# Expert gathers of a decoder block in sets of eight, with the rows of v fetched later and summed one at a time

## The chip, the cores and the metric

One core of a Trainium2 chip runs the whole kernel as one program. The metric is the device time of one execution in microseconds (us); lower is better. The core has five engines that each work through their own instructions in order: PE (matrix multiply), DVE (vector work), ACT (activations and copies), POOL (here it issues gathers) and SP (here it issues loads). DMA engines move data between the chip's memory and the core.

## What is computed

The reference is one layer of a decoder. It normalises the 1024 tokens, runs three attention branches on them, gates and adds the branches, projects, and then applies an expert layer. The change touches only the expert layer. Every token chooses 8 x 16 = 128 of 16384 experts, and an expert is one row of `u` and one row of `v`, of 1024 numbers each:

```python
def peer_ffn(h, w_q, subkeys, u, v):
    ...
    def chunk(args):
        hc, ic, gc = args
        act = jax.nn.gelu(jnp.einsum('chkd,cd->chk', u[ic], hc).astype(jnp.float32), approximate=False)
        w = (gc * act).astype(h.dtype)
        return jnp.einsum('chk,chkd->cd', w, v[ic])
```

So for each token and each of its experts: a dot product of the expert's `u` row with the token, GELU, a gate, and the `v` row times that number added to the token's output.

## The kernel before

The tokens form eight tiles of 128. Two of them (4 and 6) are done densely: `dense()` multiplies them with all 16384 experts, 128 experts at a time, in matmuls at L1221 (`uh`, `ul`, `hh`, `hl` for the dot products, `vh`, `vl`, `wh`, `wl` for the sums). For the other six tiles the rows are gathered. A gather fetches 128 rows, 0.5 MB: of 32 tokens, 4 experts each. A tile takes 128 gathers of `u` and 128 of `v`, so there are 768 of each, all issued by POOL at L1123.

`Experts.step` handles one gather. A gather of `u` lands in one of `UP` = 5 row buffers. At L1177 DVE multiplies it with the tokens' rows `hb` and sums it into one column of `parts`. `hb` holds each token's row once for every expert; `spread_rows` makes it for four gathers at a time with two matmuls into `pb` (L1116) and two copies on ACT (L128). The gather of `v` for the same experts is issued in the same step and lands in one of `VP` = 6 buffers.

Four gathers make a set. In the step after a set's last dot product, ACT takes the GELU of the set's four columns (`gel`); a step later DVE multiplies by the gates (L1191) and spreads the four columns into the weights `wz` (L1192); a step later PE does all four sums at once, 16 matmuls into `po` (L1203). These have 32 output rows each, so that four of them use a quarter of the array's columns each (`128*32` in the profile). A list called `behind` holds what the coming steps still have to do for a set. After 32 gathers, DVE adds `po` to the residual row and ACT issues the store of `row` (L1208, L1210).

ACT needs one table for `Exp` and `Ln` and another for `Gelu` and `Tanh`; when the next function needs the other table, an `ACT_TABLE_LOAD` is issued ahead of it (L126). Attention uses `Exp` and `Ln` throughout.

The program is one long stream. Attention, projections, the choice of experts and the dense part are a generator called the filler; the loop at its end puts one expert step after so much filler, by fixed costs (`LEAST`, `SLOW`, `TOKEN_NS`). The order of instructions of one engine is set when the program is built: ACT keeps the order in which the code is written, on the other engines a scheduler may move instructions by a little. In the order of PE the filler goes first through attention of the first group of tokens, then gates and projections, then the same for the next groups, then the gate matrix of the dense tiles, then the dense part, and behind that only expert steps are left.

Of the kernel before, what the change touches and what calls it, by code (L numbers as in the profile page):

```python
# [40 lines left out]
LEAST = 3000.0  # L41
SPLIT = (0,)
AHEAD = 2
UP, VP = 5, 6
GMAX = max(GROUPS)
NMAX = GMAX * 128

# [30 lines left out]
def block_kernel(ctx: ExitStack, tc: tile.TileContext, io):  # L78
# [1010 lines left out]
    def quarters(dram_tile, c):  # L1089

        return [dram_tile[32 * c:32 * c + 32, 256 * k:256 * k + 256] for k in range(4)]

    class Experts:
# [65 lines left out]
        def step(self):  # L1159

            self.supply()
            n, gT, box, g, i, ap = self.todo.pop(0)
            c, jj = divmod(g, QB)
            if i == 0:
                if jj == 4:
                    row = box["row"] = gw.tile([128, 256], F32, name="row", bufs=1)
                    for k, src in enumerate(quarters(xres[n], c)):
                        nc.sync.dma_start(row[32 * k:32 * k + 32], src)
                    if c < 3:
                        box["b"] = rows_of(n, c + 1)  # L1170
                self.spread_rows(n, box, g)
                self.hb = self.hbs.pop((n, g))
                self.parts = gw.tile([128, 4], F32, name="parts")
            self.run_behind()
            self.fetch("v", ap)
            u = self.us.pop(0)
            nc.vector.scalar_tensor_tensor(u, u, 1.0, self.hb, op0=OP.mult, op1=OP.mult,  # L1177
                                           accum_out=self.parts[:, i:i + 1])
            if i == 2 and self.todo[1:]:
                m, _, near, h, j, _ = self.todo[1]  # L1180
                if j == 0:
                    self.spread_rows(m, near, h)
            if i == 3:
                ge = gw.tile([128, 4], F32, name="gel")
                wz = gw.tile([128, 4, 32], F32, name="wz")

                def gelu(ge=ge, parts=self.parts):
                    actf(ge, parts, AF.Gelu)

                def weights(ge=ge, wz=wz):  # L1190
                    nc.vector.tensor_mul(ge, ge, gT[:, c, jj, :])  # L1191
                    nc.vector.tensor_mul(wz, ge[:, :, None].to_broadcast([128, 4, 32]),  # L1192
                                         spread[:, jj, None, :].to_broadcast([128, 4, 32]))

                def sums(i, wz=wz, box=box):
                    if "po" not in box:
                        box["po"] = pg.tile([128, 512], F32, name="po")
                    po = box["po"]
                    v = self.vs.pop(0)

                    h = 256 * (c % 2)
                    for k in range(4):
                        nc.tensor.matmul(po[32 * k:32 * k + 32, h:h + 256], wz[:, i, :],  # L1203
                                         v[:, 256 * k:256 * k + 256], start=jj == 0 and i == 0,
                                         stop=jj == QB - 1 and i == 3, skip_group_check=True)
                    if jj == QB - 1 and i == 3:
                        row = box["row"]
                        nc.vector.tensor_add(row, row, po[:, h:h + 256])  # L1208
                        for k, dst in enumerate(quarters(io["out"][n], c)):
                            nc.scalar.dma_start(dst, row[32 * k:32 * k + 32])  # L1210
                self.behind.append([gelu, weights, lambda: [sums(x) for x in range(4)]])
            return g == 31 and i == 3

        def flush(self):
# [308 lines left out]
```

## Time and profile before

| what | us |
|---|---|
| median of three runs (3707.89 to 3709.02) | 3708.14 |
| the profiled execution | 3714.9 |
| its span, first to last instruction | 3713.1 |
| PE busy | 3251.4 |
| DVE busy | 2341.3 |
| POOL busy | 1760.5 |
| ACT busy | 1354.4 |

The profiled execution took 0.18% longer than the median of the runs. PE is busy for 88% of the span and the 16 DMA engines carry 319 GB/s in the mean, but neither is an average of one kind of work: the stages differ. Attention with gathers beside it runs at 464 to 1021 us and at 1392 to 2042 us, gates and projections at 1021 to 1392 and 2042 to 2413, the gate matrix at 2413 to 2877, the dense part at 2877 to 3609, and expert steps alone from 3609 to the end. A row of a view that groups instructions has the line, the engine, the operation, the tiles as written and read, the count, and then busy time and the mean of one in ns; behind the second bar stands how long the engine was idle just before, and what ended that. For the sums (L1203) one matmul of the program is two records in the profile, so one gather is 8 records and a set of four 32.

### The profile page before, as it was taken

How to read it: one execution, taken by the hardware profiler on the slowest of the kernel's cores; microseconds unless marked ns; L12 is line 12 of the kernel's file. 1: busy time of each engine (PE TensorE's matmuls, PEld its weight loads, DVE VectorE, ACT ScalarE, POOL GpSimd, SP SyncE). 2: the span in 40 equal slices, each digit the busy share in tenths (PEclk: the TensorE clock that was granted, in tenths of full speed). 3: DMA queues.
4: the chain of work that ended last, by engine and by line, in shares of the span. 5: the costliest groups of instructions: out<-in, count | busy, mean ns of one | idle time of the engine just before them, and what ended most of it. 6: DMA issues, size and time to landing. Idle time of an engine off the chain costs nothing.

```text
span 3713.1 us, 60915 instructions
## 1 busy us (share of the span) xinstructions
PE 3251.4 (88%) x22802; PEld 2393.0 (64%) x22802; DVE 2341.3 (63%) x6153; ACT 1354.4 (36%) x2729; POOL 1760.5 (47%) x1544
## 2 busy tenths in 40 slices
PE   7999978988899888888888999875877999999984
PEld 7889755655555765655555656763556888888850
DVE  5443686455444468886555556589875777777664
ACT  4442235444311214555444222211223444444430
POOL 0000046645465455655444556445663555545556
PEclk9999989999999999999998999997988999999995
DMA  4345578889799998888977999988999999999999
GB/s 165 115 125 168 200 256 321 321 301 328 275 383 379 377 365 293 316 296 283 333 274 276 338 360 383 372 293 282 410 360 385 393 389 408 396 397 402 373 339 343
DMA packets 346431, 1185.55 MB, mean 319 GB/s; under 512 B 38744, under 2 KB 80216, under 8 KB 326680
## 3 DMA queue, kind: packets, MB, share of 16 engines
q0 software_dynamic: 221184, 805.40, 58.1%
q1 hardware_dynamic: 102672, 337.95, 24.8%
q10 hardware_dynamic: 22280, 38.31, 2.8%
q8 instruction: 180, 2.95, 0.3%
q14 instruction: 115, 0.94, 0.1%
HBM read 1142.18 MB, written 39.32 MB: 318 GB/s over the span
## 4 chain that ended last, share of the span: by engine, by line
PE 53%; DVE 16%; DMA 11%; issue 10%; ACT 4%; another core or an unknown queue 3%; POOL 3%; ACTq 1%; SPq 0%; POOLq 0%; DVEq 0%
PE bank L117 27%; PE bank L1221 17%; PE po L1203 6%; DVE u L1177 5%; DMA u<-in_u,iT 4%; DMA v<-in_v,iT 2%; POOL u L1123 1%; POOL v L1123 1%; PE pb L1116 1%; DMA b3d<-sp 1%; PE bank L121 1%; ACT e L128 1%; DMA ur<-in_uT 1%; DMA gd<-g 1%
## 5 line engine op out<-in xcount | busy, mean ns | idle before, releaser
L1123 POOL DMA_INDIRECT u<-in_u,iT x768 | 922.4, 1201 | 1137.2 <-DVE wide L339 476.9
L1123 POOL DMA_INDIRECT v<-in_v,iT x768 | 837.3, 1090 | 804.7 <-PE po L1203 588.5
L1177 DVE SCALAR_TENSOR_TENSOR u<-u,hb 128x1024 f32<-128x1024 f32 x768 | 922.9, 1221 | 465.6 <-ACT hb L128 232.7
L1203 PE MATMUL po<-v,wz 128*32 128x256 f32 x6144 | 436.6, 413 | 134.9 <-DVE wz L1192 72.4
L117 PE MATMUL bank<-wide,w 128*128 128x384 f32 x1536 | 523.5, 495 | 6.7 <-DVE sc L966 3.0
L117 PEld LDWEIGHTS bank<-wide,w 128*128 128x128 f32 x1536 | 294.4, 194 | 209.2 <-issue 19.2
L128 ACT ACTIVATE hb<-pb 128x512 f32<-128x512 f32 x384 | 209.8, 595 | 541.4 <-PE pb L1116 237.0
L1203 PEld LDWEIGHTS po<-v,wz 128*32 128x32 f32 x6144 | 184.4, 115 | 341.1 <-DVE wz L1192 93.9
L117 PE MATMUL bank<-w,wide 128*128 128x128 f32 x2304 | 273.7, 278 | 15.9 <-issue 11.7
L117 PEld LDWEIGHTS bank<-w,wide 128*128 128x128 f32 x2304 | 268.3, 194 | 25.9 <-issue 17.5
L117 PE MATMUL bank<-big,w 128*128 128x256 f32 (+1 forms) x1280 | 239.9, 343 | 8.4 <-issue 6.9
L1221 PE MATMUL bank<-hh,uh 128*128 128x256 f32 x848 | 242.7, 286 | 3.8 <-ACT uh L128 3.8
L1221 PE MATMUL bank<-hh,ul 128*128 128x256 f32 x848 | 241.0, 284 | 0.4 <-DVE ul L1301 0.4
L1221 PE MATMUL bank<-hl,uh 128*128 128x256 f32 x848 | 240.7, 284 | 0.0
L117 PEld LDWEIGHTS bank<-big,w 128*128 128x128 f32 x1280 | 209.2, 194 | 37.9 <-issue 14.0
L128 ACT ACTIVATE e<-bank 128x512 f32<-128x512 f32 (+2 forms) x208 | 109.5, 527 | 328.7 <-PE bank L117 232.7
L1221 PE MATMUL bank<-vl,wh 128*128 128x512 f32 x512 | 204.1, 399 | 10.9 <-DVE vl L1301 10.1
L1221 PE MATMUL bank<-vh,wh 128*128 128x512 f32 x512 | 203.8, 407 | 3.7 <-ACT vh L128 3.2
L1221 PE MATMUL bank<-vh,wl 128*128 128x512 f32 x512 | 200.8, 392 | 0.0
L126 ACT ACT_TABLE_LOAD x144 | 184.8, 1283 | 20.6 <-issue 12.1
L1301 DVE TENSOR_TENSOR vl<-vr,vh 128x1024 fp32r<-128x1024 f32 x128 | 157.1, 1227 | 34.0 <-ACT vh L128 28.0
L128 ACT ACTIVATE w<-bank 128x256 f32<-128x256 f32 x128 | 49.2, 385 | 336.3 <-PE bank L1221 255.0
(298 smaller groups left out, 5747.1 us busy)
## 6 DMA issues: line engine op xcount, KB each, us to landing
ur<-in_uT SPq DMA_DIRECT2D x64, 1024.0 KB
vr<-in_vd SPq DMA_DIRECT2D x64, 1024.0 KB
w<-in_w_in SPq DMA_DIRECT2D x102, 512.0 KB
w<-in_w_gate SPq DMA_DIRECT2D x72, 512.0 KB
w<-in_w_pq SPq DMA_DIRECT2D x48, 512.0 KB
g<-gd SPq DMA_DIRECT2D x16, 1024.0 KB
w<-in_w_o SPq DMA_DIRECT2D x48, 256.0 KB
w<-in_w_out SPq DMA_DIRECT2D x24, 512.0 KB
```

The lines of the kernel that those rows point to most:

```text
L117: nc.tensor.matmul(out, lhsT, rhs, **kw)
L121: nc.tensor.transpose(out, in_, ident)
L126: nc.scalar.preload_act_table_set(s)
L128: nc.scalar.activation(out, in_, f, **kw)
L1116: nc.tensor.matmul(pb, which[:, jj].rearrange("p q s -> p (q s)"), box["b3"][:, f], start=True, stop=True)
L1123: nc.gpsimd.indirect_dma_start(out=t, out_offset=None, in_=io[kind], in_offset=bass.IndirectOffsetOnAxis(ap=ap, axis=0))
L1177: nc.vector.scalar_tensor_tensor(u, u, 1.0, self.hb, op0=OP.mult, op1=OP.mult, accum_out=self.parts[:, i:i + 1])
L1203: nc.tensor.matmul(po[32 * k:32 * k + 32, h:h + 256], wz[:, i, :], v[:, 256 * k:256 * k + 256], start=jj == 0 and i == 0, stop=jj == QB - ...
L1221: nc.tensor.matmul(out, lhsT, rhs, **kw)
L1301: nc.vector.tensor_sub(lo, r[:, x], hi)
```

## The change

A set is now eight gathers. The column tile `parts` and the GELU tile `gel` have eight columns; GELU and the multiplication by the gates run once for eight gathers. The weights `wz` are still made four at a time, the second four of a set four steps after the first. The gather of `v` is issued six steps after its own `u` was used (`VLAG`), and its sum, four matmuls, runs ten steps after (`SLAG`), one gather in each step. There are six buffers for `u` and five for `v`.

```diff
-UP, VP = 5, 6
+UP, VP = 6, 5
+VLAG, SLAG = 6, 10
...
-                self.parts = gw.tile([128, 4], F32, name="parts")
+                if jj % 2 == 0:
+                    self.parts = gw.tile([128, 8], F32, name="parts")
             self.run_behind()
-            self.fetch("v", ap)
             u = self.us.pop(0)
+            at = 4 * (jj % 2) + i
             nc.vector.scalar_tensor_tensor(u, u, 1.0, self.hb, op0=OP.mult, op1=OP.mult,
-                                           accum_out=self.parts[:, i:i + 1])
+                                           accum_out=self.parts[:, at:at + 1])
...
+            def sums(at=at, i=i, jj=jj, c=c, box=box, now=self.set):
...
+                for k in range(4):
+                    nc.tensor.matmul(po[32 * k:32 * k + 32, h:h + 256], now[at // 4][:, i, :],
+                                     v[:, 256 * k:256 * k + 256], start=jj == 0 and i == 0,
+                                     stop=jj == QB - 1 and i == 3, skip_group_check=True)
...
+            self.behind.append([None] * (VLAG - 1) + [lambda ap=ap: self.fetch("v", ap)]
+                               + [None] * (SLAG - VLAG - 1) + [sums])
+            if at == 7:
+                ge = gw.tile([128, 8], F32, name="gel")
 
-                def weights(ge=ge, wz=wz):
-                    nc.vector.tensor_mul(ge, ge, gT[:, c, jj, :])
-                    nc.vector.tensor_mul(wz, ge[:, :, None].to_broadcast([128, 4, 32]),
-                                         spread[:, jj, None, :].to_broadcast([128, 4, 32]))
...
-                self.behind.append([gelu, weights, lambda: [sums(x) for x in range(4)]])
+                def scale(ge=ge, j0=jj - 1):
+                    nc.vector.tensor_mul(ge, ge, gT[:, c, j0:j0 + 2, :].rearrange("p j i -> p (j i)"))
+
+                def weights(z, ge=ge, now=self.set, j0=jj - 1):
+                    wz = now[z] = gw.tile([128, 4, 32], F32, name="wz")
+                    nc.vector.tensor_mul(wz, ge[:, 4 * z:4 * z + 4, None].to_broadcast([128, 4, 32]),
+                                         spread[:, j0 + z, None, :].to_broadcast([128, 4, 32]))
+                self.behind.insert(0, [gelu, lambda: (scale(), weights(0)), None, None, None, lambda: weights(1)])
```

Lines from 44 on are numbered one higher in the changed kernel, and later ones differ more: the sums are L1196 there, the dense matmuls L1229.

How often each engine does what, counted over the whole order of each engine:

| | before | changed |
|---|---|---|
| gathers of u, of v (POOL) | 768, 768 | 768, 768 |
| GELU of expert columns (ACT) | 192 | 96 |
| table loads (ACT) | 145 | 81 |
| products with the gates (DVE) | 192 | 96 |
| weights wz (DVE) | 192 | 192 |
| sums into po (PE, matmuls) | 3072 | 3072 |
| unbroken runs of such matmuls (PE) | 239 | 584 |
| of these ahead of the dense sums | 193 | 430 |
| among the dense sums | 39 | 147 |
| behind the last dense matmul | 7 | 7 |
| gathers summed behind the last dense matmul | 40 | 45 |

Ahead of each place of the filler the same `spread_rows` matmuls stand as before, so the steps are dealt out alike; the sums stand later.

On PE, in the dense part, before: a set of four sums stands in one piece between dense matmuls (`bank`), followed by the two `pb` matmuls for a coming set. The number behind a name tells one tile from the next.

```order
L1221 MATMUL bank_21896<-vl_26845,wh_26838 128x512
L1221 MATMUL bank_21896<-vh_26844,wl_26839 128x512
L1203 MATMUL po_25907<-v_26654,wz_26804 32x256 x4
L1203 MATMUL po_25907<-v_26746,wz_26804 32x256 x4
L1203 MATMUL po_25907<-v_26782,wz_26804 32x256 x4
L1203 MATMUL po_25907<-v_26800,wz_26804 32x256 x4
L1116 LDWEIGHTS which_83
L1116 MATMUL pb_26947<-b3_25375,which_83 128x512
```

The same engine in the dense part of the changed kernel: two sums of one gather each, with dense matmuls between them.

```order
L1229 MATMUL bank_21507<-vh_29601,wl_29596 128x512
L1196 MATMUL po_25754<-v_29500,wz_29494 32x256 x4
L1229 MATMUL bank_21504<-vh_29633,wh_29629 128x512
L1229 MATMUL bank_21504<-vl_29634,wh_29629 128x512
L1229 MATMUL bank_21504<-vh_29633,wl_29630 128x512
L1229 MATMUL bank_21505<-vh_29633,wh_29629 128x512
L1229 MATMUL bank_21505<-vl_29634,wh_29629 128x512
L1229 MATMUL bank_21505<-vh_29633,wl_29630 128x512
L1196 MATMUL po_25754<-v_29530,wz_29652 32x256 x4
L1117 LDWEIGHTS which_83
```

Where one run of sixteen matmuls stood, there are now runs of four at several places.

On ACT, in attention of the second group, before: two sets of four, each with a table load ahead of its GELU and another ahead of the next `rs` (which is `Ln` and then `Exp`).

```order
L126 ACT_TABLE_LOAD
L128 ACTIVATE gel_15180<-parts_15041 128x4
L128 ACTIVATE sq_15204<-bank_15195 128x384
L128 ACTIVATE hb_15234<-pb_15235 128x512
L128 ACTIVATE hb_15234<-pb_15238 128x512
L128 ACTIVATE sq_15252<-bank_15243 128x384
L126 ACT_TABLE_LOAD
L128 ACTIVATE rs_15256<-bank_15254 128x384
L128 ACTIVATE rs_15256<-rs_15256 128x384
L128 ACTIVATE sq_15257<-rs_15256 128x384
L126 ACT_TABLE_LOAD
L128 ACTIVATE gel_15272<-parts_15184 128x4
```

ACT at the same place of the changed kernel:

```order
L129 ACTIVATE sq_14890<-rs_14889 128x384
L129 ACTIVATE sq_14930<-bank_14921 128x384
L129 ACTIVATE hb_14952<-pb_14953 128x512
L129 ACTIVATE hb_14952<-pb_14956 128x512
L129 ACTIVATE sq_14970<-bank_14961 128x384
L129 ACTIVATE rs_14974<-bank_14972 128x384
L129 ACTIVATE rs_14974<-rs_14974 128x384
L129 ACTIVATE sq_14975<-rs_14974 128x384
L127 ACT_TABLE_LOAD
L129 ACTIVATE gel_14993<-parts_14772 128x8
```

One GELU of four columns and the pair of loads around it are gone.

On POOL, around the first gathers of the third gathered tile (its index tile is iT_11455), before: the v of a tile follows its u by five gathers of u.

```order
L1123 DMA u_11768<-in_u,iT_11455 128x1024
L1123 DMA v_11773<-in_v,iT_5663 128x1024
L1123 DMA u_11813<-in_u,iT_11455 128x1024
L1123 DMA v_11817<-in_v,iT_5663 128x1024
L1123 DMA u_11843<-in_u,iT_11455 128x1024
L1123 DMA v_11861<-in_v,iT_5663 128x1024
L1123 DMA u_11871<-in_u,iT_11455 128x1024
L1123 DMA v_11873<-in_v,iT_5663 128x1024
L1123 DMA u_11909<-in_u,iT_11455 128x1024
L1123 DMA v_11914<-in_v,iT_11455 128x1024
```

POOL at the same place of the changed kernel (the tile's index is iT_11277): five gathers of u into the tile, the gathers of v are still those of the tile before.

```order
L1124 DMA u_11565<-in_u,iT_11277 128x1024
L1124 DMA v_11571<-in_v,iT_5593 128x1024
L1124 DMA u_11574<-in_u,iT_11277 128x1024
L1124 DMA v_11580<-in_v,iT_5593 128x1024
L1124 DMA u_11619<-in_u,iT_11277 128x1024
L1124 DMA v_11627<-in_v,iT_5593 128x1024
L1124 DMA u_11653<-in_u,iT_11277 128x1024
L1124 DMA v_11659<-in_v,iT_5593 128x1024
L1124 DMA u_11669<-in_u,iT_11277 128x1024
L1124 DMA v_11675<-in_v,iT_5593 128x1024
```

The lead of u over v on POOL has grown by seven gathers: one from the deeper u buffers and six from the later fetch of v.

More of the change, by code (lines that the diff above doesn't have):

```diff
@@ L1182, in step @@
                     self.spread_rows(m, near, h)
[L1183 to L1187, printed above, removed]
-                    actf(ge, parts, AF.Gelu)
-                def weights(ge=ge, wz=wz):
-                    nc.vector.tensor_mul(ge, ge, gT[:, c, jj, :])
-                    nc.vector.tensor_mul(wz, ge[:, :, None].to_broadcast([128, 4, 32]),
-                                         spread[:, jj, None, :].to_broadcast([128, 4, 32]))
[L1195 to L1210, printed above, removed]
-                self.behind.append([gelu, weights, lambda: [sums(x) for x in range(4)]])
@@ new lines, in step @@
+            if at == 0:
+                self.set = {}
+            def sums(at=at, i=i, jj=jj, c=c, box=box, now=self.set):
+                if "po" not in box:
+                    box["po"] = pg.tile([128, 512], F32, name="po")
+                po = box["po"]
+                v = self.vs.pop(0)
+                h = 256 * (c % 2)
+                for k in range(4):
+                    nc.tensor.matmul(po[32 * k:32 * k + 32, h:h + 256], now[at // 4][:, i, :],
+                                     v[:, 256 * k:256 * k + 256], start=jj == 0 and i == 0,
+                                     stop=jj == QB - 1 and i == 3, skip_group_check=True)
+                if jj == QB - 1 and i == 3:
+                    row = box["row"]
+                    nc.vector.tensor_add(row, row, po[:, h:h + 256])
+                    for k, dst in enumerate(quarters(io["out"][n], c)):
+                        nc.scalar.dma_start(dst, row[32 * k:32 * k + 32])
@@ new lines, in step, with gelu @@
+            self.behind.append([None] * (VLAG - 1) + [lambda ap=ap: self.fetch("v", ap)]
+                               + [None] * (SLAG - VLAG - 1) + [sums])
+            if at == 7:
+                ge = gw.tile([128, 8], F32, name="gel")
+                def gelu(ge=ge, parts=self.parts, j0=jj - 1):
+                    actf(ge, parts, AF.Gelu)
+                def scale(ge=ge, j0=jj - 1):
[5 more added lines that the diff above has]
+                self.behind.insert(0, [gelu, lambda: (scale(), weights(0)), None, None, None, lambda: weights(1)])
```

## The prediction

> **What bounds the kernel now.** I read the page first, then the stretches stage by stage, then the waits, and last single moments in the order of time.
>
> ```profile
> PE 3251.4 (88%) x22802; PEld 2393.0 (64%) x22802; DVE 2341.3 (63%) x6153; ACT 1354.4 (36%) x2729; POOL 1760.5 (47%) x1544
> PE 53%; DVE 16%; DMA 11%; issue 10%; ACT 4%; another core or an unknown queue 3%; POOL 3%; ACTq 1%; SPq 0%; POOLq 0%; DVEq 0%
> ```
>
> PE is busiest (first row), and the chain of waits runs through it for half the span (second row). The rest of that chain is the loop of the expert steps and of attention through DVE, DMA and ACT. The stretches by stage show where each limit holds; their columns are the stretch, its length, busy time of PE, PEld, DVE, ACT and POOL with counts, granted clock, DMA share and GB/s.
>
> ```profile
> 464.00:1021.00 557.00, 479.08 (x3439) 313.82 (x3439) 331.77 (x884) 244.99 (x453) 297.06 (x267) 0.93 0.83 300
> 1021.00:1392.00 371.00, 337.11 (x2167) 233.62 (x2164) 183.27 (x457) 66.25 (x163) 213.00 (x196) 0.96 0.99 376
> 1392.00:2042.00 650.00, 560.89 (x4079) 370.62 (x4078) 444.57 (x1288) 318.30 (x572) 340.67 (x309) 0.93 0.83 296
> 2042.00:2413.00 371.00, 348.46 (x2249) 236.66 (x2247) 209.58 (x530) 95.02 (x268) 206.70 (x185) 0.95 0.96 363
> 2413.00:2877.00 464.00, 339.08 (x2305) 243.19 (x2301) 362.52 (x1319) 114.31 (x325) 246.53 (x218) 0.86 0.92 346
> 2877.00:3609.00 732.00, 717.51 (x5159) 600.96 (x5158) 521.76 (x827) 330.73 (x553) 387.82 (x301) 1.00 0.99 388
> 3609.00:3713.00 104.00, 46.84 (x339) 10.59 (x337) 46.98 (x90) 9.75 (x25) 67.93 (x64) 0.55 0.92 343
> ```
>
> In the dense stretch (2877 to 3609) PE is busy for 717.5 of 732 us at full clock: more PE work there is more time. In gates and projections (second and fourth row) DMA is at 0.99 and 0.96. In attention (first and third) nothing is full: PE waits for ACT and DVE between its matmuls. In the gate matrix (fifth) DVE has 362.5 of 464. The last 104 us are expert steps alone, at the pace of the gathers.
>
> ```profile
> POOL v L1123 <- PE po L1203: 588.5, 148, 19.1
> DVE u L1177 <- DMA u<-in_u,iT: 113.9, 51, 8.7
> PE po L1203 <- DVE wz L1192: 72.4, 35, 12.0
> PE po L1203 <- DMA v<-in_v,iT: 47.4, 33, 2.9
> ```
>
> The first row is the one that looks worst and counts least: POOL waits 588 us with a gather of `v` for a buffer that the sums free, but PE waits only 47.4 us for rows of `v` (last row), and the tail alone has 35.9 of those (below). The gathers of `v` are early enough now. What PE does wait for at the sums is `wz`, 72.4 us.
>
> **The change, term by term.** The span of the profiled execution is 3713.1 us and its own time 3714.9, 0.18% above the median of 3708.14. I sum against the span and move the sum to the median.
>
> *Runs of sums in the dense part, a cost.* The `po` matmuls use the array in columns of 32, the dense ones the whole of it. What a change between them costs can be read off the starts of matmuls.
>
> ```profile
> 3007.30 0.39 PE L1221 MATMUL bank<-vl,wh 128*128 128x512 f32 x1
> 3007.52 0.39 PE L1221 MATMUL bank<-vh,wl 128*128 128x512 f32 x1
> 3007.84 1.93 PE L1203 MATMUL po<-v,wz 128*32 128x256 f32 x32
> 3009.71 0.61 PE L1116 MATMUL pb<-b,which 96*128 96x512 bf16 x2
> ...
> 2875.64 0.61 PE L1203 MATMUL po<-v,wz 128*32 128x256 f32 x8
> 2876.18 0.50 PE L1221 MATMUL bank<-vh,wh 128*128 128x512 f32 x1
> 2876.52 0.40 PE L1221 MATMUL bank<-vl,wh 128*128 128x512 f32 x1
> 2876.76 0.40 PE L1221 MATMUL bank<-vh,wl 128*128 128x512 f32 x1
> ```
>
> Dense matmuls of 512 columns start 0.23 us apart (3007.30 to 3007.52, 2876.52 to 2876.76). The first `po` starts 0.32 us after the last dense one: 0.09 lost. A set of four holds PE for 1.87 us (3007.84 to 3009.71), one gather for 0.54 (2875.64 to 2876.18). Three gathers more are thus 1.33 us, 0.44 each, so 0.10 of the 0.54 is a fixed cost at the end. The first dense matmul behind it then takes 0.34 instead of 0.23, another 0.11. An isolated run costs **0.30 us** beside its body. The change breaks 39 runs among the dense sums into 147, so 108 x 0.30 = **+32 us**. PE has no idle time there to hide them; if half fell into its waits for DVE, it would be 16, and 34 is the top, with a few dense waits lengthened.
>
> [...]
>
> *Runs ahead of the dense part, a cost.* 430 instead of 193: 237 x 0.30 = 71 us of PE time. What of it is on the path I take from the share that the same matmuls have in it now.
>
> ```profile
> by line: PE bank L117 37.5%; issue 14.1%; PE po L1203 7.1%; another core or an unknown queue 7.0%; DVE u L1177 6.3%; ACT L126 2.7%; ACT e L128 2.2%; PE bank L121 2.1%; POOL u L1123 1.8%; POOL v L1123 1.5%; DMA w<-in_w_in 1.3%; PE pb L1116 1
> ...
> 464.00:1021.00 557.00, 69.42 (x1024) 31.48 (x1024) 0.93 0.83 300
> 1392.00:2042.00 650.00, 83.52 (x1216) 37.80 (x1216) 0.93 0.83 296
> ```
>
> The first row is the chain by line within 464 to 1021 us: `po` has 7.1% of 557 us, 39.5 us, of the 69.4 us that these matmuls are busy (second row): 0.57. Attention has 1024 + 1216 records, 280 of the 572 gathers ahead of the dense part, so about half of the 71 us: 34.8 x 0.57 = 20. The other half falls where DMA or DVE ends last; there I take half that share, 36 x 0.28 = 10. Together **+30 us**, between 0 and 71.
>
> *The tail, a cost.* At the last dense matmul 45 gathers are still to be summed instead of 40. On POOL five gathers more are left: six of `v` more, one of `u` less.
>
> ```profile
> L1123 POOL DMA_INDIRECT v<-in_v,iT x34 | 38.6, 1136 | 15.5 <-issue 7.9 <-PE pb L1116 3.3 <-remote 2.3
> L1123 POOL DMA_INDIRECT u<-in_u,iT x29 | 28.8, 993 | 10.7 <-issue 7.6 <-DVE gel L1191 2.2 <-DMA v<-in_v,iT 0.9
> ...
> PE po L1203 <- DMA v<-in_v,iT: 35.9, 23, 2.9
> DVE u L1177 <- DMA u<-in_u,iT: 29.8, 18, 4.0
> PE po L1203 <- DVE wz L1192: 3.2, 2, 2.3
> ```
>
> From 3609.5 on POOL issues 34 + 29 = 63 gathers in 38.6 + 15.5 + 28.8 + 10.7 = 93.6 us, 1.49 each: 5 x 1.49 = **+7 us** (0 to 8). The last three rows are waits within this tail: PE and DVE both wait for gathers, hardly for `wz`.
>
> *Waits for wz, a gain.* Of the 72.4 us, 3.2 lie in the tail; 69 remain. Now every set of four pays for the way from its last dot product over GELU, gates and spreading to the sums. Then only the first of eight does, since the second `wz` is made four steps after. I take half, **-35 us** (0 to -69). What is late next is the work behind: PE then meets the filler's own waits.
>
> *Table loads, a gain.* 64 loads fewer.
>
> ```profile
> L126 ACT ACT_TABLE_LOAD x144 | 184.8, 1283 | 20.6 <-issue 12.1 <-DVE k L587 2.7 <-DMA w<-in_w_in 2.5
> ...
> 1801.29 0.52 ACT L128 ACTIVATE sq<-rs 128x384 f32<-128x384 f32 x1
> 1801.83 1.28 ACT L126 ACT_TABLE_LOAD   x1
> 1803.13 0.20 ACT L128 ACTIVATE gel<-parts 128x4 f32<-128x4 f32 x1
> ```
>
> 64 x 1.283 = 82 us of ACT. On the chain in 464 to 1021 us the loads (`ACT L126` above) have 2.7%, 15 us, of which half goes: 8. In the other attention stage they are not among what that view lists first. I take **-10 us** (0 to -82), since ACT, busy for 245 of 557 us there, loads mostly while it would have waited for PE.
>
> [...]
>
> *One more buffer of u, a gain.* DVE waits 113.9 us for rows of `u`, less 29.8 in the tail: 84. The stages where DMA is full can gain nothing from asking earlier.
>
> ```profile
> DVE u L1177 <- DMA u<-in_u,iT: 44.8, 12, 8.7
> ```
>
> That row is of 1021 to 1392 us. Of the other 39 us I take a third, **-12 us** (0 to -84). One buffer of `v` less is covered: its gather comes after the buffer's sum of the step before.
>
> *Costed at nothing.*
>
> ```profile
> L1191 DVE TENSOR_TENSOR gel<-gel,gT x192: 135/158/232, 506.6 to 3701.7; 128x4 f32<-128x4 f32 x192
> ```
>
> 96 products with the gates fewer are 96 x 0.158 = 15 us of DVE, which is idle for 37% of the span; only in the gate matrix, where it is fullest, would its share of some 2 us show. The 192 `wz` stay.
>
> **The sum**: +32 +30 +7 -35 -10 -12 = +12 us, 0.3%. On the median: 3708.1 + 12 = **3720 us**.
>
> **The rivals.**
>
> *Attention is paced by ACT: faster.* For it: 245 and 318 us of ACT lie in two stages where PE, DVE and DMA all have room, and the loads stand between `Exp` and `Ln` that PE waits for. Then half of the 82 us comes off the path (-41 instead of -10), the runs there hide in PE's waits (0 instead of +20), and two thirds of the waits for `wz` go (-46): 12 - 31 - 20 - 11 = -50, **3658 us**. It decides from the point where the loads' share of the path passes about a quarter of their 82 us. Against it: 2.7% on the chain.
>
> *The costs cancel: no change.* Where DMA ends last (1021 to 1392, 2042 to 2413) and DVE does (2413 to 2877), neither gains nor costs of PE reach the end; +32 and +7 meet some 40 us of waits: **3708 us**.
>
> *The gains don't come: slower by more.* With one gather at a time PE meets a gather of `v` 768 times instead of finding four landed; if the waits for `wz` only turn into waits for `v`, and every run pays (+71 instead of +30), it is 12 + 35 + 41 = +88: **3796 us**. For it: DMA is at 0.92 and more in four of the stages. Against it: `v` has four steps from gather to sum, of 2413 us / 572 = 4.2 us each before the dense part, and was waited for only 11 us outside the tail.
>
> **How the numbers follow.** The forecast, slower by 0.2 to 1.5%, has 0.42, the slower rival 0.06, no change 0.16, faster 0.36. No measurement here tells less than about 0.2% (7 us) from no change. The range has to reach well into the faster rival: 3640 to 3775 us; the forecast's own range is 3715 to 3765.
>
> **What would show it.** In the changed profile: the dense stretch lengthened by 25 to 34 us with `po` runs of 8 records between dense matmuls; from the last dense matmul to the end about 111 us instead of 104; 80 or 81 table loads; waits of PE's `po` for `wz` near 35 us; POOL's wait for `po` nearly gone. If attention (1207 us now) is shorter by over 40 us, ACT was its pace and I am wrong about the sign. If the dense stretch is not longer, the 0.30 us is hidden and the forecast falls with it.

## The result, and the profile after

The changed kernel takes 3649.64 us in the median of six runs (3636.43 to 3660.02), against 3708.58 us for the kernel before beside it: 0.9843 of the time, 95% interval 0.9815 to 0.9871. It is faster by 1.6%, where the forecast was 0.3% slower.

The kernel before takes 3705 to 3710 us on most chips of this study and 3677 us on two of them, so ratios are compared, and absolute times only where that base is nearly the same. On a chip of the second kind the change gives 0.9905 (0.9873 to 0.9936). Its gain is thus 37 to 59 us, depending on the chip.

The first rows of the page of the changed kernel, busy time by engine and the chain of waits by engine:

```profile
PE 3307.4 (91%) x22802; PEld 2327.7 (64%) x22802; DVE 2332.6 (64%) x6057; ACT 1261.2 (35%) x2569; POOL 1801.6 (50%) x1544
...
PE 60%; DVE 12%; DMA 10%; issue 9%; POOL 5%; ACT 2%; another core or an unknown queue 1%; ACTq 0%; POOLq 0%; SPq 0%; DVEq 0%
```

PE has 56 us more of busy time (3251.4 to 3307.4) in a span that is 78 us shorter: it waits 134 us less. To see where, both programs are cut at the same matmuls of the filler. First the kernel before, the two attention stages, the gate matrix and the dense part (stretch, length, busy time of PE, PEld, DVE, ACT, POOL, granted clock, DMA share, GB/s):

```profile
455.90:1009.30 553.40, 474.43 (x3398) 310.42 (x3398) 334.16 (x919) 247.53 (x460) 290.52 (x262) 0.93 0.82 296
1383.70:2040.30 656.60, 567.05 (x4109) 376.19 (x4109) 443.40 (x1285) 319.03 (x572) 343.64 (x313) 0.93 0.83 298
2406.00:2878.60 472.60, 347.39 (x2373) 249.91 (x2372) 371.12 (x1354) 116.49 (x330) 252.15 (x222) 0.86 0.92 346
2878.60:3609.20 730.60, 716.12 (x5152) 599.82 (x5151) 520.36 (x823) 329.65 (x550) 386.72 (x300) 1.00 0.99 388
```

And the changed kernel, all stages from the first attention on:

```profile
454.70:983.00 528.30, 479.19 (x3343) 300.49 (x3343) 331.69 (x905) 211.00 (x418) 285.28 (x256) 0.94 0.84 304
983.00:1357.00 374.00, 353.32 (x2182) 224.30 (x2181) 186.09 (x455) 64.76 (x152) 223.80 (x197) 0.96 0.99 376
1357.00:1957.40 600.40, 563.87 (x4153) 356.30 (x4154) 440.29 (x1264) 270.77 (x516) 351.37 (x313) 0.97 0.90 324
1957.40:2324.60 367.20, 349.83 (x2182) 225.36 (x2181) 204.68 (x490) 91.92 (x253) 211.30 (x181) 0.97 0.96 366
2324.60:2776.90 452.30, 347.34 (x2357) 245.30 (x2356) 367.34 (x1338) 114.97 (x317) 258.40 (x223) 0.88 0.95 358
2776.90:3522.50 745.60, 744.94 (x5161) 585.76 (x5159) 524.78 (x809) 328.09 (x532) 396.34 (x299) 1.00 0.98 381
3522.50:3634.70 112.20, 54.33 (x378) 10.69 (x376) 44.57 (x84) 9.49 (x21) 74.26 (x69) 0.53 0.92 342
```

Length less PE's busy time is PE's idle time. In the two attention stages it falls from 79.0 + 89.6 = 169 us to 49.1 + 36.5 = 86 us, and they are 81 us shorter together (1210.0 to 1128.7). The gate matrix is 20 us shorter, its idle time falls by 20. The dense part is 15 us longer and the tail 8 (103.9 to 112.2, with the span's end at 3713.1 and 3634.7). Gates and projections stay (374.4 to 374.0 and 365.7 to 367.2 us).

The waits that the forecast spoke of, in the changed kernel (total, times, longest):

```profile
POOL v L1124 <- PE po L1196: 603.6, 272, 14.2
...
PE po L1196 <- DMA v<-in_v,iT: 77.1, 55, 5.5
...
DVE u L1179 <- DMA u<-in_u,iT: 64.9, 41, 6.7
...
PE po L1196 <- DVE wz L1217: 33.1, 9, 9.4
```

The wait for `wz` fell from 72.4 to 33.1 us as forecast, that of DVE for `u` from 113.9 to 64.9. PE's wait for rows of `v` grew from 47.4 to 77.1 us, so that its two waits at the sums together fell by only 10 us. POOL's wait for the sums did not go: 588.5 us in 148 pieces became 603.6 in 272.

### The profile page after: what moved, and what is told of

Read it like the earlier page. It is cut to its first block, busy times and chain, and to the rows that moved or that the text cites. A ratio compares the mean times of both kernels' runs of the same rounds, so it can differ in the third digit from the quotient of the medians.

```text
span 3634.7 us, 60663 instructions
## 1 busy us (share of the span) xinstructions
PE 3307.4 (91%) x22802; PEld 2327.7 (64%) x22802; DVE 2332.6 (64%) x6057; ACT 1261.2 (35%) x2569; POOL 1801.6 (50%) x1544
## 4 chain that ended last, share of the span: by engine, by line
PE 60%; DVE 12%; DMA 10%; issue 9%; POOL 5%; ACT 2%; another core or an unknown queue 1%; ACTq 0%; POOLq 0%; SPq 0%; DVEq 0%
PE bank L118 33%; PE bank L1229 17%; PE po L1196 7%; DMA v<-in_v,iT 4%; DVE u L1179 3%; POOL v L1124 3%; POOL u L1124 2%; DMA u<-in_u,iT 2%; PE pb L1117 2%; DMA ur<-in_uT 1%; DMA b3d<-sp 1%; PE bank L122 1%; DMA gd<-g 1%; DVE sc L867 1%
## 5 line engine op out<-in xcount | busy, mean ns | idle before, releaser
L1124 POOL DMA_INDIRECT v<-in_v,iT x768 | 874.1, 1138 | 816.9 <-PE po L1196 603.6
L1196 PE MATMUL po<-v,wz 128*32 128x256 f32 x6144 | 524.5, 414 | 147.8 <-DMA v<-in_v,iT 77.1
L1196 PEld LDWEIGHTS po<-v,wz 128*32 128x32 f32 x6144 | 152.6, 112 | 411.5 <-issue 168.5
L1229 PE MATMUL bank<-hh,uh 128*128 128x256 f32 x848 | 244.4, 288 | 0.3 <-issue 0.3
L1229 PE MATMUL bank<-hh,ul 128*128 128x256 f32 x848 | 240.0, 283 | 0.0
L1229 PE MATMUL bank<-hl,uh 128*128 128x256 f32 x848 | 239.8, 283 | 0.0
L1229 PE MATMUL bank<-vh,wh 128*128 128x512 f32 x512 | 213.1, 419 | 0.3 <-ACT vh L129 0.3
L1229 PE MATMUL bank<-vl,wh 128*128 128x512 f32 x512 | 200.7, 392 | 0.7 <-DVE vl L1309 0.7
L1229 PE MATMUL bank<-vh,wl 128*128 128x512 f32 x512 | 200.3, 391 | 0.0
L1229 PEld LDWEIGHTS bank<-hh,uh 128*128 128x128 f32 x848 | 162.0, 191 | 15.4 <-issue 7.8
```

Source lines behind the costliest of these rows:

```text
L1124: nc.gpsimd.indirect_dma_start(out=t, out_offset=None, in_=io[kind], in_offset=bass.IndirectOffsetOnAxis(ap=ap, axis=0))
L1196: nc.tensor.matmul(po[32 * k:32 * k + 32, h:h + 256], now[at // 4][:, i, :], v[:, 256 * k:256 * k + 256], start=jj == 0 and i == 0, stop=j ...
L1229: nc.tensor.matmul(out, lhsT, rhs, **kw)
```

## The experiments

All were run beside the kernel before on the same chip. Four theories go through them under letters. **T** is the forecast's faster rival: ACT paces attention, and fewer table loads free it. **S**: the sums taken apart are the gain. **W**: the earlier weights `wz` are. **D**, later **B**: the buffers of `v` that come free, and are filled again, four at once. With half of the gathers S is split: **S1**, a block of four sums holds PE up; **S2**, it frees four buffers at once, and gathers stand still in between. **U** is the sixth buffer of `u`. In the last three runs T stands for the traffic of the gathers. Where an expectation names a time, it took the kernel before at 3708 us.

**The sums one at a time, and nothing else.** The kernel before with

```diff
-                self.behind.append([gelu, weights, lambda: [sums(x) for x in range(4)]])
+                self.behind.append([gelu, weights] + [lambda x=x: sums(x) for x in range(4)])
```

> The kernel before with its sets of four, its 145 table loads and its five and six buffers; only the four sums of a set run in four steps instead of one (577 runs of sums instead of 239). Theory T, fewer table loads on ACT make attention shorter: no gain here, the added runs cost 10 to 40 us, so 3718 to 3750 us. Theory S, small pieces of sums fill PE's waits in attention and no longer hold the filler up: attention shorter by 50 us or more, 3640 to 3670 us. Theory W, the wait for the weights is met half as often: nothing changes in it, 3708 to 3740 us.

Measured: 0.9881 (0.9816 to 0.9945). Three rows of its stretches, cut like those above:

```profile
455.70:991.80 536.10, 477.89 (x3374) 297.09 (x3374) 336.34 (x921) 248.47 (x462) 292.52 (x260) 0.94 0.85 304
1364.90:1968.10 603.20, 563.85 (x4132) 357.18 (x4130) 443.85 (x1283) 315.62 (x568) 344.47 (x311) 0.97 0.89 321
2799.80:3544.60 744.80, 744.77 (x5161) 585.44 (x5159) 525.68 (x826) 329.74 (x551) 385.31 (x300) 1.00 0.98 381
```

Attention is 71 us shorter (1139.3 us) with 145 table loads and with sets of four. PE's idle time there is 97.6 us instead of 169, its busy time the same (1041.7 and 1041.5). The dense part is as long as in the changed kernel. The wait for `wz` hardly changed:

```profile
PE po L1203 <- DVE wz L1192: 68.8, 22, 11.9
```

So this one edit gives most of the gain, and not through a shorter wait for `wz`.

**Half of the table loads.** Every second set is copied instead of going through GELU, so that 83 loads are left:

```diff
-                    actf(ge, parts, AF.Gelu)
+                    actf(ge, parts, AF.Copy if odd else AF.Gelu)
```

> The kernel before, but every second set of four takes a plain copy instead of the GELU, so that its table loads fall from 145 to 83, about those of the change (the output of these sets is not the reference's). Sums, buffers and fetches are those of before. Theory T: attention shorter by 50 to 80 us with none of the costs in the dense part and the tail, 3625 to 3660 us. Theories S and W: no change, 3700 to 3712 us.

Measured: 0.9971 (0.9943 to 0.9999), 11 us. The attention stages are 16 us shorter (1194 us), where T asked for 50 to 80.

**The loads put back.** The changed kernel with GELU on four columns at a time, 145 loads:

```diff
+            if at == 3:
+                self.ge = gw.tile([128, 8], F32, name="gel")
+                self.behind.insert(0, [lambda ge=self.ge, parts=self.parts: actf(ge[:, :4], parts[:, :4], AF.Gelu)])
...
-                    actf(ge, parts, AF.Gelu)
+                    actf(ge[:, 4:], parts[:, 4:], AF.Gelu)
```

> The changed kernel with its GELU done four columns at a time, the first four of a set four steps ahead of the second, so that the table loads are 145 as before; weights, sums, fetches and buffers stay as in the change. Theory T: the gain goes, 3715 to 3745 us. Theories S and W: it stays, 3640 to 3665 us.

Measured: 0.9855 (0.9799 to 0.9912), against 0.9843 for the change. The gain stays with all the loads. With the run before, T is out: a table load costs ACT 1.28 us, and little of it is on the path.

**Sets of eight, sums in fours.** The changed kernel with

```diff
-UP, VP = 6, 5
-VLAG, SLAG = 6, 10
+UP, VP = 5, 6
+VLAG, SLAG = 7, 10
...
-                               + [None] * (SLAG - VLAG - 1) + [sums])
+                               + [None] * (SLAG - VLAG - 1 + 3 - i) + [sums])
```

> Sets of eight with 81 table loads as in the change, but the sums four at a time (291 runs), with five buffers of u and six of v as before and v fetched seven gathers behind. Theory T: the gain without the cost of the added runs in the dense part, 3625 to 3650 us. Theory S: as before, 3695 to 3715 us. Theory W: the gain stays, 3625 to 3655 us.

Measured: 0.9856 (0.9799 to 0.9912), attention 1154 us, dense part 723 us. This is what W expected, and S expected no gain: the kernel gains as much as the change without code that takes the sums apart. It doesn't separate the two cleanly: there are 132 runs in attention instead of 88, since the scheduler broke some sets, `wz` stands ready four steps ahead, and `v` is fetched seven gathers later. Which of these makes its gain was not tested by itself, but for the `wz`, by one step, in the next run.

**The weights one step ahead.** The kernel before, with sums and gathers of `v` a step later:

```diff
-            self.fetch("v", ap)
+            if self.late:
+                self.fetch("v", self.late)
+            self.late = ap
...
-                self.behind.append([gelu, weights, lambda: [sums(x) for x in range(4)]])
+                self.behind.append([gelu, weights, None, lambda: [sums(x) for x in range(4)]])
```

> The kernel before, with only this: the four sums of a set come one step later and the gathers of v each one step later, so that the weights wz are written two steps ahead of the sums instead of one; the sums of a set still stand together, 145 table loads stay. Theory W (the sums wait for wz at their entry, and with them everything behind on PE): the waits of PE's po for wz fall from 72 us to under 40 and the time to 3665 to 3690. Theory S (what gains is the sums taken apart, so that each little piece fills one of PE's waits for ACT and DVE): no gain, 3695 to 3720, the waits between filler matmuls in the two attention stages stay near 103 and 145 us, though the waits for wz fall.

Measured: 0.9959 (0.993 to 0.9988). The wait for `wz` is halved, and 0.4% comes of the edit; the attention stages take 1167.6 us, against 1191.5 in the kernel before on the other chip where that takes 3677 us:

```profile
PE po L1206 <- DVE wz L1195: 38.6, 15, 9.2
```

**Pairs, singles outside the dense part, and the buffers.** In the same sitting:

```diff
+                self.behind.append([gelu, weights, lambda: [sums(0), sums(1)], None, lambda: [sums(2), sums(3)]])
```

> The kernel before, with only this: the four sums of a set are taken apart in two pairs, the second pair two steps after the first; 413 runs of sums instead of 232. Theory S: more than half of the gain of the sums one at a time (which took the time to 3656), since the longest stretch in which PE serves no other engine halves: 3665 to 3685, attention 40 to 60 us shorter, dense part 6 to 10 us longer than before by the runs. Theory W: no gain, 3700 to 3715, since the first pair waits for wz as before.

```diff
+                self.behind.append([gelu, weights] + ([lambda: [sums(x) for x in range(4)]] if behind[0] else
+                                                      [lambda x=x: sums(x) for x in range(4)]))
```

> The kernel before with the sums one at a time ahead of the dense part and in the tail, and four together within it (41 runs there instead of about 145). Theory S with my price of 0.30 us a run: attention as short as with the sums one at a time everywhere (1139 us against 1210), and the dense part back at 729 to 733 us instead of 745: 3638 to 3648, faster than the changed kernel or equal to it. If the runs cost nothing in the dense part and its length comes from what is moved there: 3650 to 3660, dense part still 742 or more.

The third is the changed kernel with `UP, VP = 5, 6`.

> The changed kernel with five row buffers for u and six for v, as before, and all else of the change. If the sixth buffer of u is worth something (theory U): DVE's waits for rows of u go back from 65 to some 110 us, and the time to 3658 to 3670. If it is not: within 5 us of the changed kernel, 3645 to 3655. Rival D (with v gathered one at a time the fetches of v no longer come in bursts of four that hold up those of u): the two attention stages stay at 1125 to 1140 us here too.

Measured: the pairs 0.984 (0.9804 to 0.9875), singles outside the dense part 0.9899 (0.9866 to 0.9932), the changed kernel with the old buffers 0.9909 (0.9877 to 0.9941), all against 3676.9 us. The dense part with its sums kept in fours:

```profile
2803.00:3533.00 730.00, 715.66 (x5153) 599.68 (x5151) 521.14 (x825) 330.10 (x552) 390.91 (x299) 1.00 1.00 389
```

It is at 730 us, near the 727 of the kernel before on such a chip and not the 747 of the change (both below), so what the change loses there are the runs. The sixth buffer of `u` is worth nothing that shows (0.9909, and 0.9905 with it below). With the old buffers attention takes 1127 us, as rival D expected; S expects the same, so this run doesn't tell them apart. The pairs did better than expected.

**Both kernels again, and the two gains together.** Against 3677.28 us on one chip:

> The kernel before, unchanged, for a profile in the same sitting as the kernels below. All theories: total within 1% of 3708, the two attention stages together 1190 to 1215 us, the dense part 728 to 732, the fillers' own waits on PE in attention some 240 us.

> The changed kernel, unchanged, in the same sitting. All theories: 0.982 to 0.987 of the kernel before.

> The kernel before with only two things: the sums one at a time, and sums and gathers of v one step later, so that wz is written two steps ahead. 145 table loads, sets of four, five buffers of u and six of v stay as before. If the change's gain is the sum of its sums taken apart (0.988 alone) and of its weights ready sooner (0.996 alone): 0.982 to 0.987, as the changed kernel. If the rest of the change's gain comes from the sets of eight, its fewer loads or its buffers: 0.987 or more.

> The kernel before with the sums in pairs and sums and gathers of v one step later. If both gains add (0.984 for the pairs, 0.996 for the step): 0.978 to 0.982, the fastest of all. If the step's gain is the same waits that the pairs already take: 0.983 to 0.986.

The third is the kernel one step earlier with `[gelu, weights, None]` followed by four single sums, the fourth with two pairs, two steps apart.

| kernel | ratio | attention | gate matrix | dense | tail |
|---|---|---|---|---|---|
| before (3679.65, one run) | | 553.9 + 637.6 | 472.2 | 727.2 | 102.4 |
| changed | 0.9905 (0.9873 to 0.9936) | 520.5 + 604.8 | 455.7 | 746.6 | 111.9 |
| singly and earlier | 0.9903 (0.9871 to 0.9936) | 530.5 + 599.3 | 458.4 | 744.3 | 106.1 |
| pairs and earlier | 0.9818 (0.9789 to 0.9847) | 527.4 + 596.4 | 457.2 | 726.7 | 106.5 |

The third kernel has the old sets of four, all 145 table loads and the old buffers, and is as fast as the change: sums one at a time behind earlier weights are enough for the whole of its gain. (Against the expected 0.982 to 0.987 both fall short alike, since the change gains less on this chip.) Pairs gain as much in attention and lose nothing in the dense part; with the earlier weights they are the fastest kernel of the study that does all the work, 34 us below the changed one. Without the earlier weights they were at 0.984, and the two intervals overlap.

```profile
454.60:982.00 527.40, 476.22 (x3366) 300.69 (x3366) 333.39 (x920) 249.38 (x462) 290.78 (x260) 0.94 0.85 308
1352.00:1948.40 596.40, 561.14 (x4138) 361.38 (x4138) 443.20 (x1283) 315.71 (x568) 352.38 (x314) 0.97 0.90 326
2765.30:3492.00 726.70, 725.83 (x5153) 593.29 (x5151) 524.08 (x826) 329.20 (x550) 388.28 (x300) 1.00 1.00 390
```

Attention's idle time is 86.4 us, that of the dense part 0.9.

**Why apart is better: half of `v`'s gathers left out.** One edit, with fours and with singles:

```diff
-            self.fetch("v", ap)
+            if i % 2 == 0:
+                self.fetch("v", ap)
...
-                    v = self.vs.pop(0)
+                    v = self.vs.pop(0) if i % 2 else self.vs[0]
```

> The kernel before, with every second gather of v left out (the row of the even gather is summed twice), so that its six buffers hold three sets of four and no gather of v has to wait for sums. Output not the reference's; DMA moves a sixth less, POOL issues a quarter fewer gathers, so the time falls by 80 to 250 us whatever holds. This is the base for the next kernel: POOL's wait for po should fall from 590 to under 150 us.

> The same with the sums one at a time. Theory S1 (a block of four sums holds PE for 1.9 us, and with it PE's work for ACT and DVE): the gain of taking the sums apart stays without any shortage of v buffers: 30 to 60 us less than the kernel with sums in fours and half of v, attention 40 to 70 us shorter. Theory S2 (four sums at once free four v buffers at once, so that gathers of u stand on POOL behind gathers of v that wait): nothing is left of it, and the runs in the dense part cost 15 to 20 us: equal or slower by up to 20 us.

Measured: fours 3470.62 us, 0.9369 (0.9336 to 0.9402); singles 3508.72 us, 0.9469 (0.9439 to 0.95). Here taking the sums apart costs 38 us. Fours:

```profile
459.20:959.90 500.70, 456.46 (x3399) 300.46 (x3399) 334.36 (x921) 248.47 (x462) 232.26 (x202) 0.96 0.77 266
1312.90:1897.20 584.30, 539.93 (x4105) 364.84 (x4105) 441.92 (x1285) 318.17 (x572) 271.66 (x235) 0.96 0.78 264
2670.50:3385.90 715.40, 710.46 (x5153) 597.63 (x5152) 521.08 (x824) 328.92 (x550) 293.45 (x225) 1.00 0.93 341
```

Singles:

```profile
454.00:954.50 500.50, 462.60 (x3374) 289.32 (x3374) 334.61 (x922) 248.26 (x462) 228.29 (x200) 0.98 0.77 265
1318.20:1903.60 585.40, 560.26 (x4130) 356.59 (x4130) 442.45 (x1283) 315.76 (x569) 264.36 (x235) 0.97 0.77 261
2690.10:3434.60 744.50, 744.50 (x5161) 585.39 (x5159) 528.50 (x837) 329.52 (x551) 311.78 (x226) 1.00 0.90 330
```

With fewer gathers PE's idle time in attention is 88.6 us with fours already, instead of 169. Singles take 25.6 us of it and cost 26.5 us of busy time: nothing is gained. In the dense part, which has 4.9 us of idle time, they cost 29 us. So a piece has no value of its own. S1, which expected the gain to stay, is out; what S2 expected came out, with a loss beyond its 20 us: where gathers of `v` are early nothing is left of the gain. (POOL's wait for `po` did not fall to under 150 us in these two: it was 698 and 688, although PE waited only 16 and 10 us for rows of `v`. The likely reason is that POOL runs ahead and waits with a gather that nobody needs yet.)

**Pairs on the sets of eight.** The changed kernel with five and six buffers and each even sum, and its gather of `v`, a step later, beside its odd one.

> The changed kernel with its sums in pairs, and five buffers of u and six of v; sets of eight and 81 table loads stay. If the pairs' gain is that half of the runs and none of the dense part's 19 us are paid: 0.978 to 0.984 of the kernel before, dense part 724 to 730 us. If sets of eight are worth something beside: below the 0.982 of the pairs on sets of four.

Measured: 0.9879 (0.9834 to 0.9925), against 3706.07 us; dense part 736 us, no better than the change. The pairs on sets of four were timed only on chips where the kernel before takes 3677 us, so how much better they are on the others is open.

**Buffers or traffic.** All gathers, but the odd ones into a buffer that nobody reads:

```diff
-UP, VP = 5, 6
+UP, VP = 5, 5
...
-            self.fetch("v", ap)
+            self.fetch("v" if i % 2 == 0 else "x", ap)
```

> As the kernel with half of v and sums in fours, but with all the gathers: the odd rows of v are fetched into a sixth buffer that nobody reads, and the even ones into five (five times two sums). So POOL's issues and DMA's bytes are those of the kernel before, and the sums still come four together, but a set holds two buffers instead of four. Output not the reference's. Theory B (before, four sums at once free four buffers of v at once, and the gathers stand still in between): the gain comes without any sum being taken apart: 0.975 to 0.990 of the kernel before, attention 40 to 75 us shorter. Theory T (what matters is DMA's traffic, so that less of it was the whole help in the kernel with half of v): 0.995 to 1.005, attention as long as before.

> The same with the sums one at a time. Theory B: no gain left over the kernel with all gathers and sums in fours, a loss of 10 to 40 us by the runs (dense part 15 to 30 us longer). Theory T, or if pieces help PE by themselves when DMA is full: 30 to 50 us faster than the same with sums in fours.

Measured: 3988.65 us, 1.0744 (1.0692 to 1.0797), and 3942.6 us, 1.0625 (1.0584 to 1.0667). The pair missed its aim. Each gather into the one spare buffer waits until the one before it has landed, which is a new wait on POOL, larger than the one that was taken away:

```profile
POOL x L1123 <- DMA x<-in_v,iT: 993.3, 251, 12.5
...
POOL v L1123 <- PE po L1203: 139.2, 35, 14.3
```

Yet it shows one thing: in this kernel, where gathers are late (DVE waits 482 us for rows of `u`), taking the sums apart gains again, 46 us, 40 of them in attention (547.8 + 655.4 to 531.8 + 631.2 us).

The last run answers the question from the other side: half of `v`'s gathers, fours, and `UP, VP = 5, 3`, so that buffers are as short as before.

> The kernel with half of v's gathers and the sums in fours, with three buffers for v instead of six: a set needs two, so the buffers are as short as before (four of six), and only the bytes and issues are fewer. Output not the reference's. Theory B (short buffers, freed together, make the gaps on PE): attention nearly as long as before, 535 to 555 and 630 to 657 us, idle time of PE in the two above 140 us, total 0.96 to 0.98 of the kernel before. Theory T (fewer bytes and issues close the gaps): as with six buffers, 495 to 515 and 575 to 600 us, idle below 105 us, total 0.935 to 0.945.

Measured: 0.9428 (0.9389 to 0.9467).

```profile
465.50:981.30 515.80, 464.11 (x3398) 303.35 (x3398) 334.59 (x922) 248.21 (x462) 230.76 (x199) 0.94 0.75 255
1333.50:1920.60 587.10, 542.83 (x4109) 366.55 (x4109) 442.12 (x1285) 317.67 (x572) 267.57 (x235) 0.96 0.77 262
```

Idle time in attention is 96 us, near the 88.6 with six buffers and far from 169. It is mostly the amount of gathers that makes PE's gaps, not the buffers of `v`; those are worth some 22 us here by the ratios (0.9428 and 0.9369), with intervals that overlap. So the shortage of buffers, which S2 and B name, is at most a small part.

Through which wait a late gather reaches the filler's matmuls was not found. The chain of waits shows how much is open. Its shares by line in the second attention stage, for the kernel before, the sums one at a time, and half of `v` in fours:

```profile
by line: PE bank L117 40.0%; issue 13.7%; PE po L1203 8.2%; DVE u L1177 6.4%; another core or an unknown queue 5.0%; PE bank L121 2.0%; ACT e L128 1.9%; POOL v L1123 1.7%; POOL u L1123 1.7%; DMA u<-in_u,iT 1.4%; PE pb L1116 1.4%; DVE sc L86
by line: PE bank L117 55.9%; PE po L1203 11.6%; issue 5.6%; DMA u<-in_u,iT 3.9%; DVE u L1177 3.8%; PE pb L1116 2.4%; DMA v<-in_v,iT 2.2%; PE bank L121 1.6%; another core or an unknown queue 1.6%; ACT e L128 1.4%; DVE mx L654 0.7%; POOL u L1
by line: PE bank L117 59.3%; PE po L1204 11.5%; DVE u L1178 5.6%; issue 2.7%; PE bank L121 2.2%; PE pb L1116 2.0%; ACT e L128 1.1%; ACT rs L128 0.9%; DVE sc L866 0.8%; DVE mx L654 0.8%; DVE wide L339 0.7%; DVE sc L976 0.6%; DVE sc L974 0.6%
```

In `issue` and `another core or an unknown queue` this view names nothing of the program that was waited for. Together they have 18.7% of 656.6 us before, 123 us; 7.2% of 603.2, 43 us, with the sums apart; and 2.7% of 584.3, 16 us, with half of `v`'s gathers. In the first attention stage it is 117, 89 and 14 us. So much of what goes away is time that this view does not explain, and "PE waits for ACT and DVE" is not the whole of it. (One such piece, 10.6 us from 644.9 us on, is by the timeline POOL standing with a gather of `v` until a set has been summed.)

## Why the prediction was wrong, step by step

**The step that failed is "Runs ahead of the dense part, a cost".** It took 237 runs at 0.30 us, weighed them by the share that `po` has on the chain, and got +30 us. The price was right where it could be read, in the dense part (0.28 us a run, below). What the step left out is the other side: sums dealt out one at a time also take away waiting. The prediction had read that "PE waits for ACT and DVE between its matmuls" in attention, and it then asked how much of the new work is on the path instead of how much of the waiting goes. In the kernel with nothing but the sums taken apart, PE's idle time in attention fell by 71 us, and the stages became 71 us shorter: a gain where the step had a cost. That a piece fills the gap in which it stands fits this, and the kernels with half of `v`'s gathers, where 25.6 us of idle time were filled at a price of 26.5; but there nothing was gained, so how much of the 71 us is filled, and how much waiting never arises because rows come and go more evenly, stays open.

By the price, some 129 more runs in attention would add 39 us to PE's busy time there, and it did not grow. Most of the difference is the clock. The stretches of the kernel before around one gap, and then PE's matmuls on both sides of it:

```profile
1492.40:1495.80 3.40, 0.00 (x0) 0.00 (x0) 2.29 (x5) 2.16 (x4) 1.06 (x2) 0.99 1.02 392
1495.80:1499.20 3.40, 3.17 (x17) 2.84 (x18) 3.40 (x10) 3.35 (x5) 2.98 (x2) 0.50 0.65 204
1499.20:1502.60 3.40, 3.40 (x15) 2.43 (x14) 2.15 (x8) 1.94 (x4) 1.15 (x1) 1.00 0.85 243
```

```profile
1490.80 1.05 PE L117 MATMUL bank<-qpad,big 128*128 128x128 f32 x8
1491.69 0.38 PE L1116 MATMUL pb<-b,which 96*128 96x512 bf16 x1
1496.03 1.12 PE L117 MATMUL bank<-e,big 128*64 128x128 f32 x8 [3.96 <-ACT e L128]
1497.08 2.08 PE L117 MATMUL bank<-qpad,big 128*128 128x128 f32 x8
1498.95 0.71 PE L117 MATMUL bank<-sp,ntri 128*128 128x256 f32 x2
```

PE waits 3.96 us for `e`. While it waits, the clock is full (0.99); when it works again, the granted clock is 0.50 for 3.4 us, and then 1.00. At 0.50 the same work takes about twice as long here: eight `bank<-qpad,big` matmuls start 0.11 us apart ahead of the wait (1490.80 to 1491.69) and 0.23 behind it (1497.08 to 1498.95). So the wait is paid again in part: 3.17 us of busy time at half the clock. The granted clock of the trace has 28 such drops in the attention stages before, with 172 us, and 14 with 92 us when the sums are taken apart. PE was busy in 131 and 67 us of these, and at half the clock half of that is lost: 65 and 34 us. The stages' mean clocks in the rows above, 0.93 and 0.93 before, 0.94 and 0.97 then, agree with that; the changed kernel has 15 such drops with 96 us, and PE is busy in 72 of them. The 32 us saved here pay for most of the runs.

Each of the 28 drops before lasts 3.41 us (14 of them) or two, three or four times that. A drop often comes with a wait, but not always: of PE's 23 waits of 2 to 4 us in these stages, 14 had a drop begin during them or within 2.4 us of their end, 3 ended in a drop that had begun before them, and after 6 none began for over 20 us, among them waits of 3.24 and 3.08 us (ending at 620.1 and 927.4 us). A wait of 2.32 us was followed by one. So a filled gap can be worth more than its length; what starts a drop was not found.

The other steps:

- *Runs of sums in the dense part, +32.* The price held. A single gather's sums in the changed kernel:

```profile
3104.14 0.28 PE L1229 MATMUL bank<-hl,uh 128*128 128x256 f32 x1
3104.35 0.64 PE L1196 MATMUL po<-v,wz 128*32 128x256 f32 x8
3104.92 0.50 PE L1229 MATMUL bank<-vh,wh 128*128 128x512 f32 x1
3105.26 0.39 PE L1229 MATMUL bank<-vl,wh 128*128 128x512 f32 x1
```

  It holds PE for 0.57 us (3104.35 to 3104.92), and the next matmul takes 0.34. In this stretch 104 runs were added, and PE's busy time grew by 28.8 us (716.1 to 744.9), 0.28 each. But 13.8 us of the 14.5 us of idle time went with them, so the stage grew by only 15 us. "PE has no idle time there to hide them" was wrong by these 14.5 us, 2% of the stage.
- *The tail, +7.* 8.3 us, right.
- *Waits for `wz`, -35.* The wait fell by 39 us, as forecast. Its value alone is less: the kernel with the weights one step ahead, with nearly the same fall, gained 0.4%, 15 us. And 30 us came back as waits for rows of `v`, 22 of them outside the tail; the third rival had named this, but in the sum it was at nothing.
- *Table loads, -10.* Half of the loads taken away gave 11 us, with an interval of 0 to 21. Right, and the rival that rested on half of 82 us was wrong in its mechanism, though its 3658 us lies near the result.
- *One more buffer of `u`, -12* (a third of 39 is 13). DVE's wait fell by 49 us, and nothing of it shows in the time: without the buffer the ratio was 0.9909, with it 0.9905.
- *The gate matrix* had no term of its own. It is 20 us shorter (16.5 on the other chip), with 20 us less idle time.
- *POOL's wait for `po` nearly gone.* Wrong: it is as long as before. POOL runs ahead in both kernels and then waits for a free buffer (588.5 and 603.6 us).

The sum by stages of the two profiled executions: attention -81, gate matrix -20, dense +15, tail +8, the rest 0: -78 us of 3713.1. (By the medians it is 59; the changed kernel's profiled execution was its fastest run, 3636.43.) The test that the prediction set for itself, attention shorter by over 40 us, came out, but its reading of it, that ACT was the pace, was wrong too, as the kernels with half of the loads and with all of them show.

## What to carry to other kernels

Where an engine has gaps, work that is cut into pieces and dealt out between its waits was not simply a cost by the piece here: look at the idle time of the stage first, and set the price of the cut against it. The same cut cost 15 us where the engine is nearly full, in the dense part, and gained nothing where gathers were early, with half of `v`'s; so cut by stage, or only as fine as the gaps ask (pairs were better than singles on the two chips where both were timed). A large wait on a queue that runs ahead need not be on the path: POOL's was 590 us before, and 698 in a kernel that is 6% faster.

## What the hardware showed that was not expected

Many waits of PE were charged twice: at 14 of the 23 waits of 2 to 4 us in attention before the change, the granted clock went to 0.50, during the wait or within 2.4 us of its end, for 3.41 us or a multiple. All 28 drops there make up 65 us of lost PE time. The length of one wait does not decide it: one of 2.3 us (ending at 566.4 in the kernel before) was followed by a drop and one of 3.24 was not, and some drops came where no wait in the 7 us before was longer than 1.2 us (one starts at 1632.3).

The amount of gathers mattered far beyond the waits that name them. With 384 of 1536 gathers left out, attention is 125 us shorter, although in the kernel before the waits of DVE for rows of `u` and of PE for rows of `v` in these two stages add up to some 15 us. And the same program takes 0.8% less on some chips: its second attention stage took 656.6 us on one and 637.6 on another. Each chip was used in one sitting, so chip and sitting can't be told apart.
